# A new instruction order, and a tail with pieces of its own, in a one-core transformer layer

## The chip, the core and the metric

The kernel runs on one core of one Trainium2 chip. A core has five engines, each with an in-order queue of its own: TensorE (PE in the profile, its weight loads PEld), VectorE (DVE), ScalarE (ACT), GpSimd (POOL) and SyncE (SP), which issues the DMAs here. The metric is device time in microseconds; lower is better.

## The reference

One decoder layer on 512 tokens of width 1024, everything in float32:

```
def reference(x, ...):
    h = rms_norm(x, attn_pre_norm)
    mix = hybrid_mixer(h, ...)              # see below
    x = x + rms_norm(mix, attn_post_norm)
    h = rms_norm(x, ffn_pre_norm)
    f = (silu(h @ w_gate) * (h @ w_up)) @ w_down
    return x + rms_norm(f, ffn_post_norm)   # rms_norm: x * rsqrt(mean(x*x) + 1e-6) * gain
```

`hybrid_mixer` multiplies h by one input projection `w_in` (after which the queries and keys get rotary embedding) and feeds two groups of heads: four differential heads (the difference of two causal softmax maps of 64 dimensions, applied to 128-wide values) and eight heads of native sparse attention (NSA) in two groups, each the gated sum of a branch over 31 compressed blocks, a branch over selected blocks and a window branch. At this length every block is selected and the window covers all, so the last two are causal softmaxes over the same scores' shape with different keys. The groups are joined and go through `w_out`.

## The kernel before, in words

TensorE multiplies in a rounded 32-bit type (fp32r). So that the result keeps float32 precision, every operand is split into a high part (rounded, a ScalarE copy or POOL cast) and a low part (the rest, a VectorE or POOL subtraction), and a product is three matmuls: high by high, low by high, high by low. An operand is ready for TensorE only after the load, the high part and the low part, in that order.

There is no scheduler at run time. The program is a list of small steps, each of which appends a few instructions to the engines' queues. Two strings of names give the order of the list: `PLAN` (1384 steps) for the normalisation, input projection and attention, and `PLAN_NORM` for the output projection's norm, the feed-forward part and the end. The position of a name decides where its instructions stand in each queue, and since a queue is in order, an instruction that waits holds back all that follow it on that engine. SP's DMAs are in such a queue too.

Names in `PLAN` that matter below: `xL3`, `xH3`, `xl3` load chunk 3 of x (transposed, line L385), and make its high (L389) and low part (L393); `bL0.0` loads a block of `w_in` (L503), into a buffer that an earlier block must have left; `F m.c.k` is one product piece of the projection (L517). For the heads, D is a differential and N an NSA head: `LD` loads queries (qst, L617), `K` loads keys (`load_keys`, kst, L624), `S` are score products on TensorE (two matmuls, L867 and L868), `Q` adds the causal mask by a matmul (L873), `X` takes the row maximum (L877, VectorE), `E` the exponentials (L881, ScalarE), `R` the reciprocal of the sums and `g` the gate, `M` scales the weights by gate and reciprocal on POOL (L1050), `T` transposes them on TensorE (L898), `H` and `L` make the parts of the transposed (L908, L911), `V` are the products with the values. `SC`, `TC`, `HC` are scores (scc, L1027 with its mask at L1029), transposes (trc, L1069) and copy (pct, L1073, ScalarE) of the compressed branch. The digits behind the letters are branch or map and tile. `RB` broadcasts a row by TensorE, and `v1p2.0` is a piece of the value projection (L650). So N3S12 is a score product of NSA head 3 and D2S12 one of differential head 2; N4K0 loads the first keys of NSA head 4 over those of head 3.

In the feed-forward part gate and up projections go by a scheme with sums of operand blocks (Strassen's), so that weights are added on VectorE before the split: `load_ff.f.g` loads the gate weights of feature group f, `sum_ff.f.n` forms the sums of weights (n = 1 is L1376, e<-wraw; 2 is L1378; 3 is L1383; 4 is L1381), `high_ff`, `low_ff` split them (L1396 on ScalarE; L1404 on VectorE), `h3.s4`, `l3.s3` and the like make the high and low part of sums of activations (L1332 and L1335, in the profile "rope"), and `block.f.p` is one product of the scheme (L1419). `c0` and so on are sums of activations (L1361), `act` lines (L1438) belong to the SwiGLU of the tiles before.

In the end `down` multiplies by `w_down` (L1641), 22 feature tiles for each quarter of the output: 128 tokens (i) by 512 columns (c). The last quarter is i = 1, c = 0 (`LAST` is 1). For each i follow on the result: `last_sum` (adds the bank to the part kept so far, L1657), `last_square` (ScalarE with a running sum, L1672), `last_mean` (L1678), `last_root` (the reciprocal root of the mean square by Ln and Exp on ScalarE and a Newton step on VectorE, L299 to L308), `last_gain` (times the gain, L1687) and `last_row` (times the root, plus the residual, L1691, and the DMA to the output, L1692). The last quarter's sum and square are taken in two halves of 256 columns, out of one bank.

Of the kernel before, what the change touches and what calls it, by code (L numbers as in the profile page):

```python
# [47 lines left out]
bl1.0 F5.1.1 F4.1.1 F1.2.1 bl2.0 F0.0.1 F0.1.1 xL2 F0.2.1 xH2 F3.0.1 F5.2.1 F3.1.1 F3.2.1 F3.0.2 xl2 F2.0.2 F2.1.2  # L48
F4.0.2 bL3.0 bh3.0 F5.0.2 F0.0.2 F0.1.2 F1.0.2 F5.1.2 F0.2.2 F3.1.2 F4.2.2 xL3 xH3 F0.0.3 F5.2.2 F3.2.2 F3.0.3
F1.1.2 F1.2.2 F1.0.3 bL0.0 bh0.0 bl3.0 F3.1.3 F4.0.3 F0.1.3 xL0 xl3 xS3 F5.2.3 F5.0.3 F4.2.3 F3.2.3 F2.2.2 F2.0.3  # L50
F0.2.3 xS1 xA3 bl0.0 xH0 F0.0.0 F2.1.3 F2.2.3 xl0 F4.1.2 bL4.0 F5.2.0 bh4.0 F5.1.3 bl4.0 F1.1.3 F1.2.3 xS0 F3.0.0
F3.1.0 xL4 xH4 F4.1.3 F0.1.0 F0.2.0 F5.0.4 xl4 F2.0.0 F5.0.0 F2.1.0 F5.1.0 F5.2.4 F3.2.0 F4.0.4 F3.0.4 F3.1.4 F4.2.4
bL5.0 xL5 bh5.0 bl5.0 xH5 F4.0.5 F5.0.5 cL xl5 F2.2.0 F4.0.0 F3.2.4 xS2 F3.0.5 cc F5.1.4 xL6 xH6 xL7 F3.1.5 xl6
F4.2.0 xH7 xl7 F1.0.0 F4.1.0 KP1 F1.1.0 F1.2.0 xA2 F2.0.4 F2.1.4 F1.0.4 F0.0.4 F2.2.4 xS5 xS7 rL2 F0.1.4 F0.2.4
bL7.0 bh7.0 F4.2.7 F0.0.5 F0.1.5 F0.2.5 F1.1.4 xA5 F1.2.4 xA7 F1.0.5 F1.1.5 F1.2.5 bl7.0 F5.1.7 xS4 xA4 xS6 xA6
F5.2.5 rL0 F4.1.4 bL6.0 bh6.0 F4.2.6 rL3 xA1 rs F4.2.5 F2.0.5 KW10 bl6.0 F4.1.6 F2.1.5 F5.1.5 F2.2.5 F2.0.6 rn rb
# [25 lines left out]
N3Q02 N3X03 N2E01 W4h D1L2 D0RB N1M11 D0ML LW1 N1T02 N1H02 v1p3.0 N2R0 N2X13 N2E11 N2g0 N0O1 N0O2 N2E13 N1T01 N2CM
N2R1 N2g1 N1L02 N1H01 N1L01 N1T00 N2M00 N1H00 D1V0 D1V1 D1V2 D1O3 N1L00 N1TC N1HC N1M10 N3SC N3E03 N1T11 N2M03 pW4
D2LD0 D2S00 N3S01 N3Q01 D2Q00 N3CX N1H11 N3CA N3CE N3S1 D2X01 N3CS N2M11 N3S0 N2PH D1SQ N2M12 N4LD D2E01 W6b N2M02
D2S01 N3X02 N3E02 N1L11 N2M10 N3Q0 N3X00 N3X10 N2M01 D2X00 D2Q01 N3Q1 N3X01 N1T10 N1H10 N1L10 N2M13 N3E01 v1p3.1
D0OH N1T12 N1H12 D2S02 N3X11 N1L12 N3E00 v1a3 N3R0 D0OL D2X02 N1V00 v1d3 N1VC N3E10 N1V01 N3g0 N3CM D2E02 N1V02
N3M01 N2T00 N2H00 N2PL N3M03 N1V10 N1V11 N1V12 D2Q02 N2TC N2L00 N4SC D2LD1 D2X03 D2E00 N3PH N2T11 N4CX D2S10 N3M00
W6a N1O1 D2E03 D2S11 N2H11 D2Q10 N1O2 N2L11 D2X11 D2Q11 D2X10 N2T01 N3S11 N3E11 N3S12 W4l N3M02 N2H01 N2HC N4K0
D2S12 N2T10 D2Q12 D2E10 D2X12 N3Q12 N2L01 N3Q11 N3X12 N2T02 N3PL D2E11 D2X13 v1p2.0 W1h N2H02 N2L02 N2H10 N2L10
N2T12 N4CA D2E12 D2E13 D2R N3E12 N3X13 D2g D2MX0 D2MX3 N3E13 N3R1 N2H12 v1p2.1 N4S01 N2V00 N2V01 v1a2 D2MX2 N1OH  # L90
N4K1 N3g1 N4CE N3M13 N2VC N3M12 N2L12 N2V02 N4Q01 N3TC N3T01 N3HC N3H01 N4X02 v1d2 N4S1 D2MX1 N4S0 N3M10 N4S11 N3L01
# [162 lines left out]
def hybrid_block_kernel(  # L254
# [1400 lines left out]
    def last_sum(i, c, h=None):  # L1655
        u = piece(part[i, c], h)
        dve.tensor_tensor(u, u, piece(quarter(i, c), h), OP.add)  # L1657
# [303 lines left out]
```

## Time and profile before

| | |
|---|---|
| three runs | 627.74, 629.05, 627.74 us (median 627.74) |
| profiled execution | 628.53 us, span 626.7 us |
| TensorE | busy 614.8 us, 98% of the span |
| VectorE | 548.8 us, 88% |
| ScalarE | 374.6 us, 60% |
| POOL | 100.3 us, 16%, nearly all of it between 100 and 310 us |
| DMA | 98.41 MB, mean 157 GB/s |

The span runs from the first to the last instruction that the profiler saw; the execution's own time has some 2 us around it. The timeline gives for each instruction (or run of like ones, "x4") the start, the duration, engine, line, operation and tiles, and in brackets how long the engine had been idle before it and for what it waited. Matmuls overlap: their durations are longer than the distance of their starts, so that for TensorE the distances are read. "issue" as a reason means that nothing on another engine shows why the instruction had not begun; often it is a DMA.

### The profile page before, as it was taken

The page shows a single profiled execution, that of the slowest core. Times are in us where ns is not written, and L with a number is a line of the kernel's source. Part 1 is how long each engine was busy: PE and PEld are TensorE (multiplying, and loading weights), DVE is VectorE, ACT ScalarE, POOL GpSimd, SP SyncE. Part 2 cuts the span into 40 slices and gives each one's busy share as a digit, 9 for nine tenths or more (in the row PEclk, how much of TensorE's full clock was granted, in tenths as well). Part 3 has the DMA queues.
Part 4 walks back from the last instruction along what each step waited for, and adds up shares of the span by engine and source line. Part 5 has one row for each costly group of instructions (what it writes and reads, how often), then busy time and mean ns, then how long its engine had stood idle before and what let it go on. Part 6 is the DMA issues. An engine that isn't in the chain of part 4 may idle for free.

```text
span 626.7 us, 10975 instructions
## 1 busy us (share of the span) xinstructions
PE 614.8 (98%) x4066; PEld 558.9 (89%) x4066; DVE 548.8 (88%) x967; ACT 374.6 (60%) x783; POOL 100.3 (16%) x151
## 2 busy tenths in 40 slices
PE   9999999999999999999999999999999999999995
PEld 6888888899889989889989999999999998888884
DVE  4799798888889875999989998798999899999877
ACT  5536455558888977477574644464554656576522
POOL 0030000115878878200000000000000000000000
PEclk9999999999999999999999999999999999999998
DMA  8748887655242311545243443434442454666503
GB/s 241 247 134 287 287 283 242 224 185 169 69 153 84 135 35 35 200 169 201 65 139 101 135 136 101 135 121 150 139 136 96 132 189 147 206 220 220 172 27 134
DMA packets 38181, 98.41 MB, mean 157 GB/s; under 512 B 4208, under 2 KB 11504, under 8 KB 37232
## 3 DMA queue, kind: packets, MB, share of 16 engines
q1 hardware_dynamic: 38128, 97.72, 47.6%
q8 instruction: 32, 0.52, 0.3%
q14 instruction: 21, 0.17, 0.1%
HBM read 82.10 MB, written 15.60 MB: 156 GB/s over the span
## 4 chain that ended last, share of the span: by engine, by line
PE 85%; DVE 9%; ACT 3%; DMA 1%; issue 1%; DVEq 0%; ACTq 0%
PE yz L1419 26%; PE acc L1493 14%; PE fm L534 9%; PE fm L517 5%; PE x L1419 4%; PE v L650 4%; PE tr L898 3%; PE avn L1081 3%; PE acc L1641 3%; PE g L650 2%; PE sc L867 2%; PE sc L868 2%; PE mixp L1152 1%; DMA wraw<-in_wg 1%; PE cmp L749 1%; PE av L959 1%
## 5 line engine op out<-in xcount | busy, mean ns | idle before, releaser
L881 ACT ACTIVATE p<-sc,nm 128x384 f32<-128x384 f32 (+3 forms) x96 | 50.3, 529 | 12.8 <-DVE nm L877 11.0
L1419 PE MATMUL yz<-rope,wbh 128*128 128x256 f32 x352 | 49.2, 282 | 1.6 <-DVE rope L1335 1.6
L877 DVE TENSOR_REDUCE nm<-sc 128x1 f32<-128x384 f32 (+3 forms) x96 | 43.1, 482 | 6.5 <-PE sc L873 4.8
L1419 PEld LDWEIGHTS yz<-rope,wbh 128*128 128x128 f32 x352 | 44.9, 188 | 1.8 <-DVE rope L1335 1.8
L1050 POOL TENSOR_TENSOR p<-p,l 128x384 f32<-128x384 f32 (+3 forms) x64 | 44.8, 727 | 0.9
L911 DVE TENSOR_TENSOR ptl<-tr,pth 128x384 fp32r<-128x384 f32 (+1 forms) x60 | 34.7, 595 | 6.9 <-ACT pth L908 6.4
L908 ACT ACTIVATE pth<-tr 128x384 fp32r<-128x384 f32 (+1 forms) x60 | 30.4, 527 | 7.4 <-PE tr L898 6.7
L1404 DVE TENSOR_TENSOR wel<-e,weh 128x1024 fp32r<-128x1024 f32 x22 | 26.8, 1220 | 7.3 <-ACT weh L1396 4.2
L1396 ACT ACTIVATE weh<-e 128x1024 fp32r<-128x1024 f32 x22 | 23.3, 1057 | 14.7 <-DVE e L1378 7.7
L1396 ACT ACTIVATE wbh<-wraw 128x1024 fp32r<-128x1024 f32 x22 | 23.2, 1056 | 13.4 <-DVE wraw L1383 9.2
L898 PE MATMUL tr<-ident,p 128*128 128x128 f32 x200 | 29.8, 274 | 0.8 <-ACT pct L1073 0.5
L1396 ACT ACTIVATE whi<-wraw 128x1024 fp32r<-128x1024 f32 x22 | 23.1, 1055 | 11.4 <-DMA wraw<-in_wg 10.5
L1542 ACT ACTIVATE whi<-wraw 128x1024 fp32r<-128x1024 f32 x20 | 21.1, 1059 | 13.7 <-PE acc L1493 6.3
L1419 PE MATMUL yz<-rope,wbl 128*128 128x256 f32 x176 | 28.1, 282 | 0.0
L1404 DVE TENSOR_TENSOR wbl<-wraw,wbh 128x1024 fp32r<-128x1024 f32 x22 | 26.7, 1218 | 0.8 <-PE yz L1419 0.6
L1404 DVE TENSOR_TENSOR wlo<-wraw,whi 128x1024 fp32r<-128x1024 f32 x22 | 26.8, 1217 | 0.2 <-ACT whi L1396 0.2
L1548 DVE TENSOR_TENSOR wlo<-wraw,whi 128x1024 fp32r<-128x1024 f32 x20 | 24.1, 1219 | 1.5 <-ACT whi L1542 1.5
L1449 ACT ACTIVATE us<-yz 128x512 f32<-128x512 f32 x22 | 13.0, 593 | 19.4 <-PE yz L1419 19.3
L867 PE MATMUL sc<-kst,qst 128*128 128x512 f32 (+3 forms) x64 | 23.0, 370 | 1.3 <-issue 0.8
L898 PEld LDWEIGHTS tr<-ident,p 128*128 128x128 f32 x200 | 22.3, 141 | 1.9 <-issue 0.6
L1419 PEld LDWEIGHTS yz<-rope,wbl 128*128 128x128 f32 x176 | 23.9, 188 | 0.0
L868 PE MATMUL sc<-kst,qst 128*128 128x512 f32 (+3 forms) x64 | 21.6, 343 | 0.0
(379 smaller groups left out, 1996.2 us busy)
## 6 DMA issues: line engine op xcount, KB each, us to landing
wraw<-in_wg SPq DMA_DIRECT2D x24, 512.0 KB, 3.7
wraw<-in_wu SPq DMA_DIRECT2D x22, 512.0 KB, 3.5
wraw<-in_wd SPq DMA_DIRECT2D x22, 512.0 KB, 4.1
qk<-rope SPq DMA_DIRECT2D x7, 1024.0 KB, 5.3
kst<-qk SPq DMA_DIRECT2D x24, 256.0 KB, 4.8
wraw<-in_wf SPq DMA_DIRECT2D x10, 512.0 KB, 4.7
wraw<-in_wo SPq DMA_DIRECT2D x8, 512.0 KB, 5.1
qst<-qk SPq DMA_DIRECT2D x16, 256.0 KB, 3.6
```

The costliest lines, as they stand in the source:

```text
L534: pe.matmul(st["fm", m], fms[m][w][:, k * P:(k + 1) * P], xx[k], start=(c == 0 and k == 0), stop=(c == 2 and k == NK - 1))
L650: pe.matmul(pts[i], xx[k][:, i * P:(i + 1) * P], ws[c][wi][:, off:off + n], start=(m == 0), stop=(m == 3 * NK - 1))
L867: pe.matmul(sv[i], lhs, kk[:, 0, :w], start=(n == 0), stop=False, skip_group_check=True)
L877: dve.tensor_reduce(nm[i], sv[i], AX.X, OP.max, negate=True)
L881: act.activation(pp[i], sv[i], AF.Exp, bias=nm[i], accum_out=hs["l"][:, row, i:i + 1])
L898: pe.transpose(tr[:, n * P:(n + 1) * P], pp[i][:, j * P:(j + 1) * P], ident)
L911: dve.tensor_tensor(part(u, 1), tv[u], f32(part(u, 0)), OP.subtract)
L1050: pool.tensor_tensor(p, p, hs["l"][:, 1 + br, i:i + 1].to_broadcast(list(p.shape)), OP.mult)
L1396: act.activation(t[0], w[src], AF.Copy)
L1404: dve.tensor_tensor(t[1], W[f][PARTS[n][0]], f32(t[0]), OP.subtract)
L1419: pe.matmul(o, W[f][w][wi][:, k * P:(k + 1) * P], hop[h][hi][:, k * HS:(k + 1) * HS], start=(n < 3 and m == 0), stop=(m == 11), skip_group ...
L1493: pe.matmul(acc[t], a[x][:, t * P:(t + 1) * P], b[y], start=(first and n == 0), stop=(last and n == 2))
```

## The change

Four edits come together.

1. Steps 31 to 868 of `PLAN` are put in another order. The steps are the same. This reaches from the second chunk of x to N4K0; from `D2Q12` on the orders are equal.
2. In `PLAN_NORM` the step `l3.s3` moves ahead of `sum_ff.4.1`.
3. The last reciprocal roots: one ScalarE function `Abs_reciprocal_sqrt` in place of Ln and Exp, and the Newton step in another form, with one VectorE operation fewer and a ScalarE copy beside it. The table that is loaded for it changes.
4. The end of the last quarter. `down` for it stops at feature tile 19, and tiles 20 and 21 are multiplied in halves of 256 columns into two banks of their own (`down_piece`). The sum becomes a 512-wide addition for the first bank and a 256-wide one for each piece. `last_gain` of half 1 of `LAST` goes to POOL. The last row goes out in three pieces (512, 256 and 256 columns), the last of them by a DMA that ScalarE issues. Squares of tile 0 are written into the same scratch as those of `LAST`, and the order at the end is another.

```diff
+    def rsqrt_last(outp, ss, scale, rest):
+        v, y, t, z = (cpool.tile([P, 1], F32, tag=f"rr{j}c", name="rr", bufs=2) for j in range(4))
+        act.activation(y, ss, AF.Abs_reciprocal_sqrt, bias=rest, scale=scale)
+        dve.tensor_scalar(v, ss, scale, rest, OP.mult, OP.add)
+        dve.scalar_tensor_tensor(t, y, y, v, OP.mult, OP.mult)
+        act.activation(z, y, AF.Copy, scale=-0.5)
+        dve.scalar_tensor_tensor(outp, t, 3.0, z, OP.subtract, OP.mult)
...
-                      start=(first and n == 0), stop=(f == NF - 1 and n == 2))
+                      start=(first and n == 0), stop=(f == (NF - 3 if (i, c) == (LAST, 0) else NF - 1) and n == 2))
+
+    def down_piece(f, h):
+        o = HS + LAST % 2 * P
+        for n, (a, wi) in enumerate(((0, 0), (1, 0), (0, 1))):
+            pe.matmul(accs[7][h][:, :HS], ffx[f][a][:, o:o + P], piece(oa[f]["w"][wi][:, CS[0]], h),
+                      start=(f == NF - 2 and n == 0), stop=(f == NF - 1 and n == 2))
...
     def last_sum(i, c, h=None):
         u = piece(part[i, c], h)
-        dve.tensor_tensor(u, u, piece(quarter(i, c), h), OP.add)
+        dve.tensor_tensor(u, u, quarter(i, c) if h is None else accs[7][h][:, :HS], OP.add)
...
-        rsqrt_mean(r, wc[i][0][:, j:j + 1], 1.0 / D_MODEL, "c", wc[i][0][:, 3:4])
+        rsqrt_last(r, wc[i][0][:, j:j + 1], 1.0 / D_MODEL, wc[i][0][:, 3:4])
...
-        dve.tensor_tensor(out_tiles(i)[1 + c], part[i, c], gains[2][:, CS[c]], OP.mult)
+        u = out_tiles(i)[1 + c]
+        (nc.gpsimd if (i, c) == (LAST, 1) else dve).tensor_tensor(u, part[i, c], gains[2][:, CS[c]], OP.mult)
...
-    def last_row(i, c):
-        u = wc[i][1 + c]
-        dve.scalar_tensor_tensor(u, u, wc[i][3], x2[i][:, CS[c]], OP.mult, OP.add)
-        nc.sync.dma_start(out[i * P:(i + 1) * P, CS[c]], u)
+    def last_row(i, c, h=None):
+        u = piece(wc[i][1 + c], h)
+        dve.scalar_tensor_tensor(u, u, wc[i][3], piece(x2[i][:, CS[c]], h), OP.mult, OP.add)
+        (nc.scalar if h else nc.sync).dma_start(piece(out[i * P:(i + 1) * P, CS[c]], h), u)
...
-snap_2.3 sx.1 block.2.3 h3.s3 load_ff.4.u low_ff.3.b block.3.3 sum_x.3 load_ff.4.g high_ff.4.a sum_ff.4.1 l3.s3
+snap_2.3 sx.1 block.2.3 h3.s3 load_ff.4.u low_ff.3.b block.3.3 sum_x.3 load_ff.4.g high_ff.4.a l3.s3 sum_ff.4.1
...
-table.natural_log_exp_and_others cut_b.3.0.1 load_b.8 cut_b.4.1.0 cut_b.4.1.1 cut_b.4.2.1 load_s4.4 cut_b.8.2.0
+table.abs_reciprocal_sqrt_and_small cut_b.3.0.1 load_b.8 cut_b.4.1.0 cut_b.4.1.1 cut_b.4.2.1 load_s4.4 cut_b.8.2.0
```

Behind the first functions all line numbers of the new kernel are larger, by 8 in the middle and by up to 15 at the end.

TensorE at the end of the reordered stretch, before: the scores of NSA head 3 (kst_1117), those of differential head 2 (kst_2083), then transposes.

```order
L867 MATMUL sc_2293<-kst_1117,qst_1878 128x384
L868 MATMUL sc_2293<-kst_1117,qst_1878 128x384
L867 MATMUL sc_2298<-kst_1117,qst_1878 128x512
L868 MATMUL sc_2298<-kst_1117,qst_1878 128x512
L867 MATMUL sc_2308<-kst_2083,qst_2245 128x512
L868 MATMUL sc_2308<-kst_2083,qst_2245 128x512
L898 MATMUL tr_2311<-ident_83,p_1960 128x128
```

The same place in the new order (head 3's keys are kst_1056, those of differential head 2 kst_1745):

```order
L875 MATMUL sc_2280<-kst_1056,qst_1908 128x384
L876 MATMUL sc_2280<-kst_1056,qst_1908 128x384
L875 MATMUL sc_2283<-kst_1745,qst_2148 128x512
L876 MATMUL sc_2283<-kst_1745,qst_2148 128x512
L875 MATMUL sc_2287<-kst_1056,qst_1908 128x512
L876 MATMUL sc_2287<-kst_1056,qst_1908 128x512
L906 MATMUL tr_2298<-ident_83,p_1972 128x128
```

The pair D2S12 has gone from behind to ahead of N3S12, which is the last to read head 3's keys.

VectorE in the feed-forward part, before: around the sums of the weights of group 4 (e<-wraw waits for their load) and the low part that `l3.s3` makes (rope<-s_4132).

```order
L1335 TENSOR_TENSOR rope<-s_4075,rope 128x4x128
L1438 TENSOR_TENSOR act_4166<-x_3894,snap 128x256
L1404 TENSOR_TENSOR wbl<-wraw,wbh 128x1024
L1438 TENSOR_TENSOR act_4196<-x_3970,snap 128x256
L1376 TENSOR_TENSOR e<-wraw 128x512
L1335 TENSOR_TENSOR rope<-s_4132,rope 128x4x128
L1378 TENSOR_TENSOR e<-wraw,e 128x512
L1404 TENSOR_TENSOR wlo<-wraw,whi 128x1024
```

The same place in the new order:

```order
L1343 TENSOR_TENSOR rope<-s_4075,rope 128x4x128
L1446 TENSOR_TENSOR act_4166<-x_3894,snap 128x256
L1412 TENSOR_TENSOR wbl<-wraw,wbh 128x1024
L1446 TENSOR_TENSOR act_4196<-x_3970,snap 128x256
L1343 TENSOR_TENSOR rope<-s_4132,rope 128x4x128
L1384 TENSOR_TENSOR e<-wraw 128x512
L1386 TENSOR_TENSOR e<-wraw,e 128x512
L1412 TENSOR_TENSOR wlo<-wraw,whi 128x1024
```

The two neighbours rope<-s_4132 and e<-wraw have changed places.

VectorE's last instructions before, from the row of half 0 of tile 0 on (c_7131 is half 1 of the last tile, c_7172 half 0):

```order
L1657 TENSOR_TENSOR c_7131<-c_7131,acc_6630 128x512
L1691 SCALAR_TENSOR_TENSOR uf<-uf,rs,x2b_7094 128x512
L1687 TENSOR_TENSOR uf<-c_7131,gain 128x512
L1691 SCALAR_TENSOR_TENSOR uf<-uf,rs,x2b_7094 128x512
L1657 TENSOR_TENSOR c_7172<-c_7172,acc_6698 128x256 x2
L1678 TENSOR_SCALAR ss<-ss 128x1 x2
L1687 TENSOR_TENSOR uf<-c_7172,gain 128x512
L300 TENSOR_SCALAR rr<-ss 128x1
L303 SCALAR_TENSOR_TENSOR rr<-rr 128x1
L307 TENSOR_SCALAR rr<-rr 128x1
L308 TENSOR_TENSOR rs<-rr 128x1
L1691 SCALAR_TENSOR_TENSOR uf<-uf,rs,x2b_7335 128x512 x2
```

And in the new order:

```order
L1671 TENSOR_TENSOR c_7131<-c_7131,acc_6630 128x512
L1671 TENSOR_TENSOR c_7172<-c_7172,acc_6698 128x512
L1671 TENSOR_TENSOR c_7172<-c_7172,acc_6679 128x256
L1692 TENSOR_SCALAR ss<-ss 128x1
L1671 TENSOR_TENSOR c_7172<-c_7172,acc_6680 128x256
L1702 TENSOR_TENSOR uf<-c_7172,gain 128x512
L1692 TENSOR_SCALAR ss<-ss 128x1
L299 TENSOR_SCALAR rr<-ss 128x1
L300 SCALAR_TENSOR_TENSOR rr<-rr 128x1
L302 SCALAR_TENSOR_TENSOR rs<-rr 128x1
L1706 SCALAR_TENSOR_TENSOR uf<-uf,rs,x2b_7335 128x512
L1706 SCALAR_TENSOR_TENSOR uf<-uf,rs,x2b_7335 128x256 x2
```

The gain of half 1 has left the queue (it is POOL's), the sum of half 0 is three operations, the gain of half 0 stands ahead of the second mean, and the rows of the tile before stand ahead of these.

More of the change, by code (lines that the diff above doesn't have):

```diff
@@ L47 @@
 wu xL1 gc xH1 xl1 bL1.1 bh1.1 F2.0.1 F4.2.1 F1.0.1 F4.0.1 bl1.1 bL1.0 bh1.0 F5.0.1 F1.1.1 F2.1.1 F2.2.1 bL2.0 bh2.0
[L48 to L56, printed above, removed]
@@ L82 @@
[L82 to L91, printed above, removed]
@@ new lines @@
+N2S12 N0VC N0V10 N3S0 D1H2 N0V11 N1M11 N0L12 N0V12 N2X11 N2Q12 N2X10 N2E10 D1T1 N2S11 D1L0 D1V0 D1L2 N0O1 N1M10 D1H1
+N1M03 N0O2 D1L1 N2E11 N3SC N3Q0 N2CS N2E01 N2X13 N2E13 N3CX D1V1 D1V2 D1O3 N2Q11 N1TC N1HC N3X10 N2R0 N2X12 N2g0
+N2M03 N3X00 D0RB D0ML N1T00 N2CM N2E12 N2R1 N2g1 N1T10 N1H10 N1T01 v1p3.0 N1H01 N3E10 N1L01 D2S01 N1T02 D2Q01 N3CA
+D0OH N1T12 N1L10 N2M02 v1p3.1 N2M11 D1SQ N3CE N3CS D2S00 N3E00 N3S01 N3S1 N1H02 N1L02 N1H12 N1L12 N2M00 N2PH N2PL
+v1a3 D2LD1 D2X02 N1H00 N1L00 v1d3 D2E02 N3S02 N1T11 N1H11 N3Q01 N3X02 N3E02 N3Q02 N3Q1 N3X01 N3E01 D2Q00 N1V00 N1VC
@@ new lines @@
+N1V01 D2S02 N3X03 N3E03 N1L11 N1V02 N2M13 N2M12 D2X01 D2Q02 D2X03 N2T11 D2X00 N2H11 D0OL D2E03 N1V10 N1V11 N1V12
+N1O1 N2M01 N2M10 N2L11 N2T00 N2H00 N3R0 N3X11 N3E11 N3g0 N2T01 N2H01 N3CM N1O2 N2L00 D2S10 D2S11 N4LD N4SC N4CX N2TC
+D2Q11 D2Q10 N3S11 D2S12 N3M01 N3S12 D2X11 D2E01 N2HC D2X10 N2T10 N3M03 W6b W6a N3PH N3M00 D2E00 N4K0 N3M02 D2Q12
+D2E10 D2X12 N3Q12 N2L01 N3Q11 N3X12 N2T02 N3PL D2E11 D2X13 v1p2.0 W1h N2H02 N2L02 N2H10 N2L10 N2T12 N4CA D2E12 D2E13
+D2R N3E12 N3X13 D2g D2MX0 D2MX3 N3E13 N3R1 N2H12 v1p2.1 N4S01 N2V00 N2V01 v1a2 D2MX2 N1OH N4K1 N3g1 N4CE N3M13 N2VC
@@ L1663, in out_tiles @@
             wc[i] = [cpool.tile([P, 4], F32, tag="ssc", name="ss", bufs=NT), sslot("uf", F32), sslot("uf", F32)]
-            if i == LAST:
+            if not junk and i in (0, LAST):
                 junk.extend(sslot("uj", BF16) for _ in range(2))
@@ L1670, in last_square @@
         j = (1 - c) + (h or 0)
-        sq = junk[c] if i == LAST else wc[i][1 + c].bitcast(BF16)
+        sq = junk[c] if i in (0, LAST) else wc[i][1 + c].bitcast(BF16)
         act.activation(piece(sq[:, :SEQ], h), piece(part[i, c], h), AF.Square,
@@ L1794, in hybrid_block_kernel @@
     at(-1.0, table, "silu_and_others")
-    at(te + 6.0, table, "natural_log_exp_and_others")
+    at(te + 6.0, table, "abs_reciprocal_sqrt_and_small")
     D = 3 * 2 * 0.228
```

125 lines of the change are left out of this document (70 added, 55 removed).

## The prediction

> **What bounds the kernel now.** I read the page first (shares, chain, costliest groups), then the busy time by stretches, then the timeline of TensorE wherever a stretch showed idle time, and the engines that it waits for there. The page and the stretches:
>
> ```profile
> PE 614.8 (98%) x4066; PEld 558.9 (89%) x4066; DVE 548.8 (88%) x967; ACT 374.6 (60%) x783; POOL 100.3 (16%) x151
> PE 85%; DVE 9%; ACT 3%; DMA 1%; issue 1%; DVEq 0%; ACTq 0%
> ```
>
> ```profile
> 0.00:160.00 160.00, 158.78 (x924) 137.76 (x925) 133.00 (x257) 91.11 (x201) 22.18 (x38) 1.00 0.70 229
> 160.00:190.00 30.00, 28.20 (x213) 25.69 (x212) 25.62 (x60) 25.64 (x74) 24.50 (x37) 1.00 0.33 109
> ```
>
> TensorE is the bound: 98% busy, 85% of the chain. So an edit can pay in two ways only: it closes a hole in TensorE's row, or it shortens the 7 us after its last matmul. The first 160 us have 1.22 us of idle (mostly the start, ahead of the first product), and the next 30 us have 1.80; the new order of the attention part covers these 190 us. That already bounds the gain of the large edit: some 2 us, not 20. Its harm has no such bound.
>
> **The new order of the attention part.** Holes are read from start to start, since a matmul's end is modelled. Three are inside the stretch that is reordered or just behind it:
>
> ```profile
> 167.05 0.23 PE L1029 MATMUL scc<-cmask_b,ident_b 128*128 128x128 bf16 x1
> 167.79 0.52 PE L898 MATMUL tr<-ident,p 128*128 128x128 f32 x3 [0.51 <-ACT pct L1073]
> ...
> 177.44 0.23 PE L1029 MATMUL scc<-cmask_b,ident_b 128*128 128x128 bf16 x1
> 177.51 0.50 PE L898 MATMUL tr<-ident,p 128*128 128x128 f32 x3
> 178.44 0.30 PE L867 MATMUL sc<-kst,qst 128*128 128x128 f32 x1 [0.43 <-ACT p L881]
> ```
>
> ```profile
> 180.19 0.40 PE L867 MATMUL sc<-kst,qst 128*128 128x512 f32 x1
> 180.66 0.39 PE L867 MATMUL sc<-kst,qst 128*128 128x512 f32 x1
> ...
> 181.13 0.60 PE L898 MATMUL tr<-ident,p 128*128 128x128 f32 x4
> ...
> 183.50 0.49 PE L898 MATMUL tr<-ident,p 128*128 128x128 f32 x3
> 183.75 0.72 PE L650 MATMUL v<-whi,xh 128*128 128x256 f32 x4
> 184.30 0.64 PE L650 MATMUL v<-whi,xl 128*128 128x256 f32 x4
> 184.78 0.64 PE L650 MATMUL v<-wlo,xh 128*128 128x256 f32 x4
> 186.21 0.41 PE L867 MATMUL sc<-kst,qst 128*128 128x384 f32 x1 [0.79 <-issue]
> ```
>
> ```profile
> 180.85 2.37 SPq L624 DMA_DIRECT2D kst<-qk  x4
> ```
>
> A (167 us): from the mask product to the transposes 0.74, against 0.07 for the same pair at 177.44: 0.67 lost to ScalarE's copy of the transposed compressed weights (L1073), with only the scc group between. In the new order N1TC is followed by D0RB and by N1T00, N1T10 and N1T01, and the scc group N3SC has gone ahead of it. I take this hole as closed, -0.67 (0 if ScalarE is as late for the next transposes).
> B (178 us): 177.51 to 178.44 is 0.93, where three transposes take 0.25 (183.50 to 183.75): 0.68 lost to an exponential that still holds a bank. Its neighbours change places; I count half, -0.34 (0 to -0.68).
> C (186 us): the keys of NSA head 4 (N4K0, four DMAs on SP) can only go when N3S12, the pair of 180.19, has read the old ones: SP issues at 180.85, and TensorE stands at 186.21, 1.43 after 184.78 where such a group takes 0.48 (184.30 to 184.78): 0.95 lost. "issue" hides a DMA here. Now the diff shows that D2S12, the pair of 180.66 to 181.13, stands ahead of N3S12 instead of behind it. All else between N3S12 and N4S01 is the same work, so 0.47 us of cover leaves this gap and the hole should grow from 0.95 to 1.42: +0.47, on the path. Only a faster load would undo it.
> Elsewhere the old order has next to no holes in 160 us, so the new one can only make some. What was moved furthest upstream is the load of x's chunk 3, behind block bL0, which waits for a buffer. It goes out where chunk 0 did:
>
> ```profile
> 6.71 0.58 PE L517 MATMUL fm<-xh,whi 128*128 128x512 f32 x1
> ```
>
> ```profile
> 8.60 0.72 ACT L389 ACTIVATE xh<-xraw,gc 128x512 fp32r<-128x512 f32 x1
> ```
>
> ```profile
> L385 SPq DMA_DIRECT2D xraw<-in_xT x1: 542/542/542, 8.1 to 8.1; - x1
> DMA to landing us min/median/max: 4.1/4.1/4.1
> ...
> xraw<-in_xT SPq DMA_DIRECT2D x8, 256.0 KB, 5.4
> ```
>
> The rows: TensorE's first product, the rounding of a chunk, the load of chunk 0, and the median of all eight. Issued at 8.1 and landed at 12.2, rounded by ScalarE in 0.72 until 12.95; the first product with it is the 30th after the start at 6.71, which at 0.23 a product falls at about 13.4. So it just fits, and with the median landing of 5.4 TensorE would wait 0.8. For all such new waits I take +0.3, with bounds 0 and +2.0 (a handful of holes of the size of A to C).
>
> **The swap of l3.s3 and sum_ff.4.1.** VectorE, ScalarE and SP around 318 us, and TensorE there:
>
> ```profile
> 318.09 0.69 DVE L1376 TENSOR_TENSOR e<-wraw 128x512 f32<-128x512 f32 x1 [1.87 <-DMA wraw<-in_wg]
> 318.70 0.68 DVE L1335 TENSOR_TENSOR rope<-s,rope 128x512 fp32r<-128x512 f32 x1
> 319.90 1.22 DVE L1404 TENSOR_TENSOR wlo<-wraw,whi 128x1024 fp32r<-128x1024 f32 x1
> ```
>
> ```profile
> 317.25 0.63 PE L1419 MATMUL yz<-rope,wbh 128*128 128x256 f32 x4
> 319.44 0.74 PE L1419 MATMUL yz<-rope,wbh 128*128 128x256 f32 x4 [1.56 <-DVE rope L1335]
> 321.44 0.64 PE L1419 MATMUL yz<-x11h,wlo 128*128 128x256 f32 x4
> 321.93 0.75 PE L1419 MATMUL yz<-rope,wbh 128*128 128x256 f32 x5
> ```
>
> ```profile
> 317.99 1.06 ACT L1396 ACTIVATE whi<-wraw 128x1024 fp32r<-128x1024 f32 x1 [2.28 <-DMA wraw<-in_wg]
> ```
>
> VectorE stands 1.87 us before L1376 for a weight load, with the rope operand that TensorE needs behind it in the queue. Moved ahead it runs at 316.2 to 316.9, while VectorE idles anyway, and TensorE goes on at 317.72. But of the hole of 1.72 (317.25 to 319.44 less 0.47) only a part is won, because the block's second half needs the same load. TensorE would finish its two rope groups at 318.7 and wait until 319.1 for whi, which ScalarE can't start before the landing; then x11h and x11l on whi until 320.0, and wlo, on VectorE now at 319.3 (one operation of 0.60 less ahead of it) to 320.5, costs another 0.5. The group after it starts at 321.0 instead of 321.93: -0.9 (bounds -0.3, if a later load holds the next block up, and -1.7).
>
> **The tail.** Last matmul at 619.25, then VectorE and ScalarE alone:
>
> ```profile
> 615.62 0.15 DVE L1678 TENSOR_SCALAR ss<-ss 128x1 f32<-128x1 f32 x1 [0.19 <-ACT uf L1672]
> 615.70 0.68 DVE L1687 TENSOR_TENSOR uf<-c,gain 128x512 f32<-128x512 f32 x1
> ...
> 619.68 0.75 DVE L1657 TENSOR_TENSOR c<-c,acc 128x256 f32<-128x256 f32 x2
> 620.81 0.68 DVE L1687 TENSOR_TENSOR uf<-c,gain 128x512 f32<-128x512 f32 x1
> 621.08 0.30 ACT L299 ACTIVATE rr<-ss 128x1 f32<-128x1 f32 x1
> ...
> 622.36 1.41 DVE L1691 SCALAR_TENSOR_TENSOR uf<-uf,rs,x2b 128x512 f32<-128x512 f32 x2
> ```
>
> ```profile
> L1050 POOL TENSOR_TENSOR p<-p,l 128x384 f32<-128x384 f32 (+3 forms) x64 | 44.8, 727 | 0.9
> ```
>
> ```profile
> L1140 POOL TENSOR_TENSOR wl<-wraw,wh 128x512 fp32r<-128x512 f32 x10 | 12.7, 1286 | 0.2
> ...
> out<-uf SPq DMA_DIRECT2D x4, 256.0 KB, 2.0
> ```
>
> VectorE has no gap from 614 on, so what counts is its queue. The gain of half 1 goes to POOL (-0.60, as a 512-wide operation takes from start to start, 318.09 to 318.70); the sum over tiles 18 and 19 is a new 512-wide addition (+0.60): nil together. The first root now follows both gains without the 0.19 of idle, so VectorE comes to it at 616.1 instead of 616.3, and it is a little shorter: the rows behind it start about 0.24 earlier. The halves of the last sum no longer wait for each other's matmuls but still for VectorE: I get the last 256-wide sum done at 620.3, gain until 620.9, mean until 621.2, the root function 621.5 (0.30, as Ln's), then two VectorE steps of a quarter us, with the Copy beside the first, where the stretch between 621.38 and 622.36 held Exp and three steps: rows from 622.0 instead of 622.36, three pieces in the same 1.4. Gain 0.3. The last store is issued by ScalarE; it and two queues are not in the trace: bounds -0.6 and +0.5, I take -0.3. The new bank of pieces costs twelve 256-wide products at 0.12 for six at 0.23, nil. The table load stays one of three.
> Weighed against this: the Trainium skill ("DMA: Bandwidth & Descriptors", Anatomy of one DMA) gives a transfer's time as 2.0 us and bytes over 436e9. By that, an estimate from its figures, a last piece of 128 KB instead of 256 KB saves another 0.3 us and the whole would be 626.0. The trace's 2.0 us for 256 KB doesn't bear the sum out (2.6 by the rule), so I don't count it.
>
> **The sum.** -0.67 - 0.34 + 0.47 + 0.3 - 0.9 - 0.3 = -1.4 us. The profiled execution took 628.53 us with a span of 626.7, 0.8 above the median of the runs shown (627.74, up to 629.05), so I set the change against the median: 626.3 us.
>
> **Rivals.**
> No measurable change (627.2, between 626.5 and 629.0): the swap gives 0.3 to 0.6 since the wait for its load turns up at the next block, A only moves, C grows. For it: TensorE catches up with the same load twice within 3 us. Against: nothing after 320 us shows a hole of that size. Chance 0.36. A measurement of this kernel can tell about 0.2%, 1.26 us, from no change, so my forecast lies just past that edge.
> The tail's POOL gain. POOL would start it when the sum of half 1 ends, about 618.9, and by 1.29 (L1140) end at 620.2, 0.1 us before VectorE's last gain. If the two exclude each other, each 0.1 us that POOL is later is lost once, at most 1.29: by 0.3 the tail's gain is gone and the time is 626.6. The Trainium skill ("SBUF — State Buffer", Who interferes with whom) states such a lock: a VectorE operation with both inputs in SBUF and a GpSimd operation that reads SBUF block each other for a whole instruction. No row of the tail can show it, since POOL does nothing there now. Chance that it costs over 0.3: 0.1, counted within the other cases.
> Slower (629.5): POOL's scaling of the NSA weights. It is busy 24.50 of 30 us in 160 to 190. N2T11 now comes 9.6 us of TensorE work behind N2's last exponential, with six scalings between (at 0.73 from L1050, 4.4 us) and the reciprocal and gate, which I put at 1: some 4.2 us to spare. If POOL is further behind than that, TensorE waits for the rest, one for one; the sign turns when the backlog passes 4.2 + 1.4, and at 7.4 it is 1.8 slower. For it: POOL has only 5.5 idle us here. Against: most scalings were emitted well ahead. Chance 0.12.
> The change doesn't do what it says in the tail, where VectorE stays the chain and the new addition eats what POOL takes over; that is in the sum already. All holes closed with no new one would give -0.67 - 0.68 - 0.9 - 0.6, and +0.47: 625.4; chance 0.14, within faster.
>
> **Chances and range.** Forecast and its better case 0.52 together, no change 0.36, slower 0.12. The range goes from 624.6, the better case with the whole hole of 1.7 at 318 us, to 628.6, where the new waits reach 2.0 and the swap gives 0.3.
>
> **What would show it.** The swap: L1335's second rope operation near 316.2, and TensorE with two short waits, for whi and wlo, instead of 1.56. C: the wait for kst about 0.5 longer. A: no wait for pct near 167. The start: no wait for x's chunk 3 near 13.4. Tail: rows from 1.0 us after the last mean, no wait for POOL. I am wrong if TensorE shows new waits of more than 1 us before 190 us, or if the gain at 318 us is gone by 330.

## The result, and the profile after

The changed kernel takes 624.32 us in the median of six runs (622.59 to 625.94) against 628.51 us for the kernel before (six runs, 627.74 to 629.05): a ratio of 0.9933, 95% interval 0.9918 to 0.9948, so 4.2 us faster (3.3 to 5.2). The profiled execution is the fastest of the six, 622.59 us with a span of 620.5; against the trace of before (628.53, span 626.7) it shows 6.2 us, more than the medians do. Every ratio below is to the kernel before, run beside the kernel in question on the same chip. Two of the executions below were disturbed (669.9 us with the new order alone, and 1228.5 us, the profiled one, in the kernel with distances by phase); the times given leave them out, and that profile is not read.

The page's busy times and then the busy time by stretches after the change (the first stretch from 20 us on), to be laid beside those of before:

```profile
PE 610.4 (98%) x4072; PEld 555.3 (89%) x4072; DVE 548.8 (88%) x964; ACT 374.1 (60%) x783; POOL 101.6 (16%) x152
```

```profile
20.00:160.00 140.00, 139.56 (x844) 124.19 (x843) 122.52 (x234) 78.85 (x183) 25.63 (x37) 1.00 0.66 225
160.00:190.00 30.00, 29.93 (x234) 28.18 (x233) 27.29 (x65) 26.51 (x79) 22.15 (x35) 1.00 0.34 107
```

The 1.80 us of idle in 160 to 190 us have become 0.07. But TensorE's *busy* time has fallen by 4.4 us as well, with the same work (six 512-wide products have become twelve 256-wide ones, hence 4072 for 4066). No edit of the four takes a product away; this is what the prediction had no term for. Where it went is seen when the trace is cut at four instructions of TensorE: the first product of the projection, the first and the last Strassen product (L1419, 1848 of them), and the last matmul.

| us | first product at | to first Strassen product | Strassen products | to last matmul | to the end |
|---|---|---|---|---|---|
| before | 6.71 | 280.01 | 224.84 | 107.69 | 7.45 |
| after | 6.25 | 278.32 | 220.52 | 108.03 | 7.38 |
| difference | -0.46 | -1.69 | -4.32 | +0.34 | -0.07 |

The first column went from 5.9 to 7.4 us over the traces below whatever the kernel. The third is the surprise. Its Strassen products, before (start, duration; four matmuls in a row):

```profile
363.30 0.64 PE L1419 MATMUL yz<-x22h,dh 128*128 128x256 f32 x4
363.77 0.63 PE L1419 MATMUL yz<-x22l,dh 128*128 128x256 f32 x4
364.24 0.64 PE L1419 MATMUL yz<-x22h,dl 128*128 128x256 f32 x4
364.72 0.64 PE L1419 MATMUL yz<-xs1h,weh 128*128 128x256 f32 x4
365.19 0.64 PE L1419 MATMUL yz<-xs1l,weh 128*128 128x256 f32 x4
```

And the same products after:

```profile
359.88 0.62 PE L1427 MATMUL yz<-x22h,dh 128*128 128x256 f32 x4
360.33 0.62 PE L1427 MATMUL yz<-x22l,dh 128*128 128x256 f32 x4
360.78 0.62 PE L1427 MATMUL yz<-x22h,dl 128*128 128x256 f32 x4
361.24 0.64 PE L1427 MATMUL yz<-xs1h,weh 128*128 128x256 f32 x4
361.71 0.64 PE L1427 MATMUL yz<-xs1l,weh 128*128 128x256 f32 x4
```

Four x22 products took 0.47 us from start to start and now take 0.45 (113 ns each instead of 118); four xs1 products take 0.47 to 0.48 in both. Nothing waits. What tells the two kinds apart is where their operands lie: the root function has four columns instead of three, each in two slots of 32 bytes, so the pool of constants grew by 64 bytes per partition and all pools behind it (weights, s, r) lie 64 bytes further on; pools a and b, laid out from the other end, do not move. The distance of the stationary operand's start from the moving operand's, modulo 256 bytes (from the addresses in the two programs), and the mean time from start to start:

| moving, stationary (pools) | products | before: distance, ns | after: distance, ns |
|---|---|---|---|
| xs1, xs2 with weh, wel (a, a) | 528 | 0, 119.6 | 0, 119.7 |
| x22 with dh, dl (a, s) | 264 | 128, 118.8 | 192, 115.0 |
| x11, x12 with whi, wlo (b, weights) | 528 | 128, 118.8 | 192, 115.4 |
| rope with wbh, wbl (r, a) | 528 | 128, 118.7 | 64, 116.0 |

Only the pairs whose distance changed got faster. The granted TensorE clock doesn't tell the two traces apart: its mean is 0.997 of full speed before and 0.996 after. Theory P: the distance of the two operands sets the pace, and the gain is mostly this. Theory L: the pace is set by how a block of products happens to begin, and the order or chance changed that.

### The profile page after: what moved, and what is told of

The parts are those of the page before. It is cut to its first block, busy times and chain, and to the rows that moved or that the text cites. A ratio compares the mean times of both kernels' runs of the same rounds, so it can differ in the third digit from the quotient of the medians.

```text
span 620.5 us, 10979 instructions
## 1 busy us (share of the span) xinstructions
PE 610.4 (98%) x4072; PEld 555.3 (89%) x4072; DVE 548.8 (88%) x964; ACT 374.1 (60%) x783; POOL 101.6 (16%) x152
## 4 chain that ended last, share of the span: by engine, by line
PE 94%; DVE 2%; DMA 1%; ACT 1%; POOL 1%; issue 0%; DVEq 0%; ACTq 0%
PE yz L1427 30%; PE acc L1501 14%; PE fm L542 9%; PE mix L1174 5%; PE x L1427 5%; PE fm L525 4%; PE tr L906 4%; PE acc L1649 3%; PE avn L1089 3%; PE g L658 2%; PE v L658 2%; PE sc L875 2%; PE sc L876 2%; PE mixp L1160 1%; PE cmp L757 1%; PE av L967 1%
## 5 line engine op out<-in xcount | busy, mean ns | idle before, releaser
L889 ACT ACTIVATE p<-sc,nm 128x512 f32<-128x512 f32 (+3 forms) x96 | 50.4, 530 | 16.2 <-DVE nm L885 15.7
L1702 POOL TENSOR_TENSOR uf<-c,gain 128x512 f32<-128x512 f32 x1 | 1.3, 1282 | 359.2 <-DVE c L1671 359.2
L1058 POOL TENSOR_TENSOR p<-p,l 128x256 f32<-128x256 f32 (+3 forms) x64 | 45.2, 732 | 1.0
L875 PE MATMUL sc<-kst,qst 128*128 128x512 f32 (+3 forms) x64 | 22.7, 365 | 0.0
```

The costliest lines, as they stand in the source:

```text
L875: pe.matmul(sv[i], lhs, kk[:, 0, :w], start=(n == 0), stop=False, skip_group_check=True)
L889: act.activation(pp[i], sv[i], AF.Exp, bias=nm[i], accum_out=hs["l"][:, row, i:i + 1])
L1058: pool.tensor_tensor(p, p, hs["l"][:, 1 + br, i:i + 1].to_broadcast(list(p.shape)), OP.mult)
```

## The experiments

**64 bytes alone, and everything but the 64 bytes.**

```diff
     eps = cpool.tile([P, 1], F32, name="eps")
+    shift = cpool.tile([P, 16], F32, name="shift")
+    dve.memset(shift[:, :1], 0.0)
```

> The kernel before with one unused tile of 64 bytes per partition among the constants and nothing else; every tile of the left-hand pools (weights, s, r) lies 64 bytes further on, as in the changed kernel. Theory P (placement): the 256-wide products whose moving and stationary operands lie in pools of different sides go from 118.8 to about 115.5 ns start to start, so 2 to 4 us faster than before, with the holes near 167, 178, 186 and 318 us as they were. Theory L (the pace is set by how each block of products happens to begin, or by the order): within 0.5 us of before and a pace of 118.8 to 119.6 ns for all pairs of pools.

Measured: 625.37 us against 628.15, ratio 0.9961 (0.9944 to 0.9978): 2.5 us faster (1.4 to 3.5) by an unused tile. The pairs' paces are 119.7, 114.9, 115.3 and 116.2 ns, in the order of the table, and the x22 products run as in the changed kernel:

```profile
365.24 0.62 PE L1421 MATMUL yz<-x22h,dh 128*128 128x256 f32 x4
365.69 0.62 PE L1421 MATMUL yz<-x22l,dh 128*128 128x256 f32 x4
366.14 0.62 PE L1421 MATMUL yz<-x22h,dl 128*128 128x256 f32 x4
```

The Strassen products take 220.69 us, 4.15 less than in the trace of before; the other stretches of this trace are longer by 0.86 in sum. The holes of the old order are still there (waits of 0.5, 0.45 and 1.2 us at 168, 179 and 187 us).

The other way round, on the changed kernel:

```diff
-        v, y, t, z = (cpool.tile([P, 1], F32, tag=f"rr{j}c", name="rr", bufs=2) for j in range(4))
+        v, y, t, z = (cpool.tile([P, 1], F32, tag=f"rr{j}c", name="rr", bufs=2 if j < 2 else 1) for j in range(4))
```

> The changed kernel with its four small root columns in six slots instead of eight, so that all other tiles lie where they lay in the kernel before. Theory P: the pace is back at 118.8 ns and above, and 2 to 2.5 us of the gain are left (order 1.7, swap 0.6, tail 0 to 0.3), so 2 to 4 us slower than the changed kernel. Theory L: as the changed kernel, 4 us faster than before.

Measured: 627.01 us, ratio to before 0.9987 (0.9974 to 1.0001), paces 118.6 to 119.6 ns, and four x22 products take 0.47 to 0.48 us again:

```profile
362.95 0.63 PE L1427 MATMUL yz<-x22h,dh 128*128 128x256 f32 x4
363.42 0.64 PE L1427 MATMUL yz<-x22l,dh 128*128 128x256 f32 x4
363.90 0.64 PE L1427 MATMUL yz<-x22h,dl 128*128 128x256 f32 x4
```

So order, swap and tail together are worth 0.8 us (0 to 1.6), less than the 2 to 2.5 that I still expected of them, and the place of the tiles the rest of the 4.2, some 3.4, beside the 2.5 (1.4 to 3.5) that it gave alone. The order as a cause falls, and chance with it: same order, same tail, other distances, other pace. What is left of theory L is taken up below.

**All distances in one kernel, and distance 0.** Pool a's slots 4128 instead of 4096 bytes apart:

```diff
-        return A.tile([P, D_MODEL], dt, tag="f", name=name, bufs=NF4)
+        return A.tile([P, D_MODEL + 8], dt, tag="f", name=name, bufs=NF4)[:, :D_MODEL]
```

> The changed kernel with the sixteen feed-forward tiles of pool a laid out 4128 bytes apart instead of 4096, so that their start takes all eight multiples of 32 bytes modulo 256, and each pair of stationary and moving operand has one of eight distances. Theory P (the distance of the two operands' starts modulo some power of two sets the pace): a table of pace by distance, about 119.6 ns at 0, 118.8 at 128, 115 to 116 at 64 and 192, whatever the pools. Theory Q (it is the pools or the time that matter, not the distance): one pace for each pair of pools at all distances.

Measured: 625.10 us in a single execution, and by distance 118.6 ns at 0, 118.5 at 32, 116.7 at 64, 118.2 at 96, 118.2 at 128, 118.3 at 160, 117.1 at 192, 117.7 at 224. Pairs inside pool a reach 117.2 at 64 and 192 as the pairs across pools do: it is the distance, not the pool. Nor is it where one operand lies by itself: distance 64 gave 116.5, 117.1 and 117.3 ns with the moving operand's start at 64, 32 and 96 bytes modulo 128, while distance 0 with both at 64 gave 118.6. The spread is smaller than between whole layouts; why is not shown.

Another 64 bytes of constants on the changed kernel (the unused tile of the first experiment, with `eps`), which makes every Strassen distance 0:

> The changed kernel with another unused tile of 64 bytes among the constants, so that the left-hand pools lie 128 bytes further than in the kernel before and most pairs start at distance 0 modulo 256. Theory P: the pace of all pairs is 118.5 to 120 ns as at distance 0 in pool a, and the gain of placement is gone: 0 to 1 us faster than before. Rival: any move away from the old place helps, as fast as the changed kernel.

Measured: 627.78 us, ratio 0.9985 (0.9972 to 0.9999). All 1848 run at 120.0 ns in the mean, to be read off the rows:

```profile
360.41 0.64 PE L1429 MATMUL yz<-x22h,dh 128*128 128x256 f32 x4
360.89 0.64 PE L1429 MATMUL yz<-x22l,dh 128*128 128x256 f32 x4
361.37 0.64 PE L1429 MATMUL yz<-x22h,dl 128*128 128x256 f32 x4
361.85 0.64 PE L1429 MATMUL yz<-xs1h,weh 128*128 128x256 f32 x4
```

The forecast holds for the pace and missed one thing: the stretch from the last Strassen product to the last matmul took 106.21 us instead of 108.03. The 512-wide products of that stretch are fastest in this layout. Before, and in this kernel:

```profile
564.16 0.40 PE L1493 MATMUL acc<-whi,tbh 128*128 128x512 f32 x1
564.40 0.40 PE L1493 MATMUL acc<-whi,tbl 128*128 128x512 f32 x1
564.63 0.39 PE L1493 MATMUL acc<-wlo,tbh 128*128 128x512 f32 x1
564.86 0.39 PE L1493 MATMUL acc<-whi,tbh 128*128 128x512 f32 x1
```

```profile
556.40 0.39 PE L1503 MATMUL acc<-th,sh 128*128 128x512 f32 x1
556.63 0.39 PE L1503 MATMUL acc<-th,sl 128*128 128x512 f32 x1
556.86 0.39 PE L1503 MATMUL acc<-tl,sh 128*128 128x512 f32 x1
557.08 0.39 PE L1503 MATMUL acc<-th,sh 128*128 128x512 f32 x1
```

Three steps of the first take 0.70 us, three of the second 0.68; by pairs of pools the mean is 228 to 232 ns before, where the distances are mixed (228 to 229 for the pairs at distance 0, 232 for those at 128), and 226.7 at distance 0 throughout (227.7 for one pair of pools).

**The new order alone, twice, and the changed kernel without it.** `PLAN` of the changed kernel in the kernel before:

> The kernel before with the new order of the attention part alone (tiles where they were). If the two traces split rightly, 1.3 to 2.2 us faster than before: the holes at 167, 178 and 186 us gone, the one at 318 us as before, the pace of the 256-wide products as before. If order and pace hang together (theory L): 3 to 5 us faster.

Measured: 628.30 us, ratio 1.0001 (0.9986 to 1.0017), twelve runs from 625.91 to 630.40. The holes at 167, 178 and 186 us are gone (29.68 us of 30 busy in 160 to 190) and two others have come; for the larger one, TensorE's row and ScalarE's name the cause:

```profile
73.30 2.12 PE L534 MATMUL fm<-xh,whi 128*128 128x512 f32 x8 [1.09 <-ACT whi L521]
```

```profile
70.95 1.06 ACT L737 ACTIVATE whi<-wraw 128x1024 fp32r<-128x1024 f32 x1 [3.11 <-DMA wraw<-in_vw]
72.19 1.06 ACT L521 ACTIVATE whi<-wraw 128x1024 fp32r<-128x1024 f32 x1 [0.18 <-DMA wraw<-in_wf]
```

ScalarE stands 3.11 us before the split of the value compression's weights, and the split that the projection needs is queued behind. In the changed kernel's trace, in the same order, that load lands in time:

```profile
68.65 1.06 ACT L745 ACTIVATE whi<-wraw 128x1024 fp32r<-128x1024 f32 x1 [0.23 <-DMA wraw<-in_vw]
70.36 1.06 ACT L529 ACTIVATE whi<-wraw 128x1024 fp32r<-128x1024 f32 x1 [0.65 <-DMA wraw<-in_wf]
```

The load went out at 63.3 and 63.5 us in the two, among nine DMAs within 6 us, and the two loads of its kind took 8.1 and 6.3 us in the median to land. So the order alone was run again:

> The new order alone at the old places, once more, since its first trace showed two weight loads landing late (1.26 us at 71.8 us, 0.74 at 89.9) that the same order does not show in the changed kernel. If that was chance: 1.5 us less between the first product and the first Strassen product, and a median 0.5 to 1.5 us below before. If it belongs to the order: the same holes at the same places, and no gain.

Measured: 627.14 us, ratio 0.9972 (0.9955 to 0.9989); the hole at 72 us is 0.66 this time, and another at 139 us is 0.73. And the changed kernel with the old order:

> The changed kernel with the attention part's old order. If the order is worth what the profile of the changed kernel shows (the holes at 167, 178, 186 us closed), 1.5 to 2 us slower than the changed kernel, 0.4% faster than before. If the new order's own late loads eat that on average, as its run alone suggests, the same as the changed kernel, 0.6 to 0.7% faster than before.

Measured: 624.87 us, ratio to before 0.9946 (0.9925 to 0.9967), beside 0.9933 with the new order. From the first product to the first Strassen product, eight traces with the old order took 279.3 to 280.4 us (mean 279.8), seven with the new one 277.9 to 280.8 (mean 279.1). The new order is some 1.6 us better in the four traces in which its loads land in time (277.9 to 278.6) and no better or worse in the three in which they don't (279.6 to 280.8), 0.8 us on average of these traces. The pairs of medians (0.55 here, 0.53 and 0.82 below, -0.15 and 1.29 alone) lie within their noise but for the last, whose interval is clear of no change.

**The swap alone, twice.**

```diff
-snap_2.3 sx.1 block.2.3 h3.s3 load_ff.4.u low_ff.3.b block.3.3 sum_x.3 load_ff.4.g high_ff.4.a sum_ff.4.1 l3.s3
+snap_2.3 sx.1 block.2.3 h3.s3 load_ff.4.u low_ff.3.b block.3.3 sum_x.3 load_ff.4.g high_ff.4.a l3.s3 sum_ff.4.1
```

> The kernel before with l3.s3 ahead of sum_ff.4.1 and nothing else. TensorE's wait of 1.56 us gives place to two of 0.6 and 0.4: 0.6 to 0.9 us faster. Rival: the next load takes it back by 330 us, 0 to 0.3 us.

> The swap alone once more, since in its first trace TensorE waited 0.9 + 0.4 us for the high and low parts of the same weight load, against 0.4 in all with the changed kernel's other parts. If the landing of that load varies by chance: a wait between 0.4 and 1.3 us and a gain between 0.2 and 1.2 us. If it is fixed by the code around: again 1.3 us and a gain of 0 to 0.3 us.

Measured: 627.72 us, ratio 0.9998 (0.9988 to 1.0008), then 627.40, 0.9986 (0.9974 to 0.9998). TensorE's wait of 1.56 for rope is gone in both; it waits 0.9 and 0.4 us for whi and wlo in the first, 0.4 and 0.4 in the second. The wait that takes its place is for the same load, whose landing varies. So does the wait that the swap removes: in the five readable traces without the swap it is 0.7 to 1.6 us (1.3 on average), and in the ten with it the two waits sum to 0.2 to 1.3 (0.8 on average). The 1.56 of the trace before lies near the upper end.

**The tail alone.** The old order, the old places, the swap undone in the changed kernel:

> The changed kernel with the old order of the attention part, with l3.s3 back behind sum_ff.4.1, and with the root columns in six slots: the new tail alone at the old places. By the profiles, from the last matmul to the end 7.4 us against 7.45 before: 0 to 0.3 us faster. Rival: the tail holds what the order and the swap did not give, 0.6 to 1 us faster.

Measured: 628.63 us, ratio 1.0013 (0.9996 to 1.0030); from the last matmul to the end 7.40 us against 7.45. The tail gives nothing that can be measured here.

**All Strassen products at 64 or 192, with both orders.** Each slot of pool a 128 bytes longer, weh and wel 64 bytes into theirs:

```diff
-    def f4(name, dt=F32):
-        return A.tile([P, D_MODEL], dt, tag="f", name=name, bufs=NF4)
+    def f4(name, dt=F32, off=0):
+        return A.tile([P, D_MODEL + 32], dt, tag="f", name=name, bufs=NF4)[:, off:off + D_MODEL]
...
-            t = pair_of("w" + n)
+            t = tuple(f4(f"w{n}{h}", F32R, 16 if n == "e" else 0) for h in "hl")
```

> The changed kernel with pool a's tiles 4224 bytes apart and the sums of gate and up weights (weh, wel) starting 64 bytes into theirs, so that all 1848 Strassen products have their two operands 64 or 192 bytes apart modulo 256. Theory P (distance sets the pace): the 528 products that stayed at 119.7 ns go to 115 to 116 ns and the others gain by the even pace, 2 to 4 us faster than the changed kernel (1.0% to 1.3% faster than before); the down products, whose distances get more mixed, lose at most 0.5 us. Rival: only the pairs across pools follow the distance, and no more is to be had.

> The kernel just named with the attention part's old order. If the new order is worth its 1.5 us between the first product and the first Strassen product, 1.5 us slower than that; if late loads take it back in half of the executions, 0.5 to 0.8 us.

Measured: 622.97 us, ratio 0.9921 (0.9895 to 0.9947) with the new order and 623.50, 0.9920 (0.9905 to 0.9936) with the old. The xs products went from 119.7 to 116.4 ns, about as forecast (115.8 at 64, 116.8 at 192), but x22's rose from 115.0 to 117.5 and the mean only fell from 116.8 to 116.2. The x11 and x12 products kept their distance of 192 and went from 115.4 to 116.6, so a product's own distance is not all.

The means hide two paces. In the changed kernel's trace, the groups of four products at distance 64 or 192 run either at 113 to 114 ns each (167 of 320 groups) or at 116 to 119 (153), and none between. Two groups at distance 192, in this trace:

```profile
384.09 0.63 PE L1427 MATMUL x<-x12l,whi 128*128 128x256 f32 x4
384.56 0.63 PE L1427 MATMUL x<-x12h,wlo 128*128 128x256 f32 x4
...
387.90 0.62 PE L1427 MATMUL yz<-x11h,whi 128*128 128x256 f32 x4
388.36 0.62 PE L1427 MATMUL yz<-x11l,whi 128*128 128x256 f32 x4
388.81 0.62 PE L1427 MATMUL yz<-x11h,wlo 128*128 128x256 f32 x4
```

Four products take 0.47 us in the first and 0.45 to 0.46 in the second. It is not chance: 313 of 318 groups run at the same pace in the trace with the attention part's old order. In the layout of this experiment, with every product at 64 or 192, only 157 of 447 groups are at the fast pace; before, at distance 0 or 128, no group is under 116. So the distance decides whether the fast pace occurs, and which of the two a stretch runs at is settled by something that stays the same from run to run, as theory L had it in part; what it is, is not shown.

The two kernels of this experiment have the fastest medians of the study, 0.8 to 1.4 us under the changed kernel's; the intervals overlap with its 0.9933, so that they beat it is likely and not shown.

**Each phase with its own distances.** The kernel of distance 0 with pool r and the four tiles of pool b moved:

```diff
+    rpad = R.tile([P, 16], F32, name="rpad", bufs=1)
+    dve.memset(rpad[:, :1], 0.0)
...
-... else B.tile([P, D_MODEL], dt, tag=n, name=n, bufs=1) for n in (name + "h", name + "l"))
+... else B.tile([P, D_MODEL + 64], dt, tag=n, name=n, bufs=1)[:, 16:16 + D_MODEL] for n in (name + "h", name + "l"))
```

> The kernel shifted by 128 with pool r and the four tiles of pool b moved 64 bytes, so that 1056 of the Strassen products have distance 192 (64 the other way round) and the other 792 and all down products distance 0. Theory P, each phase by its own distances: Strassen products of about 116 ns in the 1056 and 119.5 ns in the 792, 221 to 222 us for that phase against 225.5 at distance 0, and the down products at 226.7 ns as there, 106.2 us for what follows against 108.0 of the changed kernel: 1.0 to 1.2% faster than before. Rival: the pace of the down products hangs on something else that the even layout had, and comes back to 229 ns with pool b moved: 0.7% faster.

> The kernel just named with the attention part's old order, the third pair that differs in the order alone. From the pairs so far (0.55, 0.53 us for the new order, and 0.15 against and 1.3 for it when it stood alone): 0.5 us slower than the kernel just named, with less spread from run to run.

Measured: 624.99 us, ratio 0.9948 (0.9930 to 0.9966) with the new order, 625.81, 0.9959 (0.9941 to 0.9977) with the old. The trace with the old order shows 117.9 ns in the 1056 moved products, 120.0 in the 792 others, and 226.7 to 228.1 ns in the 512-wide ones, 106.27 us for their stretch. So each phase follows its own distances. The 256-wide gain was half of what I expected: all 257 groups of four at distance 192 run at the slower of the two paces, 117 to 119 ns, and none at 113. Why is not shown.

## Why the prediction was wrong

It forecast 626.3 us, 1.4 less than before, and 624.6 at the lowest. Measured was 624.32, which is 4.2 less than the kernel before that ran beside it (628.51, where I set out from 627.74). The sign was right; the size was not, since the largest term was missing.

The step that failed is the one that says that an edit can pay in two ways only, by closing a hole in TensorE's row or by shortening the 7 us after its last matmul. It read "98% busy" as a floor and put a change of TensorE's busy time at nothing, without a reason. That time fell from 614.8 to 610.4 us. The same step shows in the part on the tail, where the root's new form was counted as instructions only: its fourth column also costs 64 bytes of the constants, which move three pools, and this is worth 2.5 us alone and 3.4 as the difference between the changed kernel and the same with six slots. The starts of before could have raised the question: nearly all lie between 113 and 122 ns apart for one shape.

Without the 64 bytes the changed kernel takes 627.01 us, 0.9987 of before (0.9974 to 1.0001), which can't be told from the rival "no measurable change". So the right sign is in the main luck: it was won by a term that the prediction didn't have.

The terms that I did have, order, swap and tail, sum to -1.4 in the text; the kernel with exactly these three took 0.8 us less than before (0 to 1.6). One by one:

- A and B, -0.67 and -0.34: closed in all seven readable traces of the new order, the changed kernel's among them. A stands at 0.5 us of wait in all eight traces of the old order, as told. B comes and goes there, being absent in three of the eight.
- C, +0.47: wrong in sign. I took the load of head 4's keys to go over head 3's, and so to be released by N3S12. That holds before; the program has two slots for keys, and in the new order this load takes the one of differential head 2, which D2S12 releases, the pair that had moved ahead. Again the load goes out behind the first of the two pairs, 4.4 us of TensorE's work ahead of its use, so the cover is what it was. And the hole has closed:

```profile
178.83 0.40 PE L875 MATMUL sc<-kst,qst 128*128 128x512 f32 x1
...
183.40 0.64 PE L658 MATMUL v<-wlo,xh 128*128 128x256 f32 x4
183.88 0.34 PE L875 MATMUL sc<-kst,qst 128*128 128x384 f32 x1
```

```profile
179.49 2.37 SPq L632 DMA_DIRECT2D kst<-qk  x4
```

  In the old order TensorE goes on 0.09 us after the second of the four DMAs has landed, in all eight traces. From issue to landing, that DMA before and after:

```profile
L624 SPq DMA_DIRECT2D kst<-qk x1: 599/599/599, 181.3 to 181.3; - x1
DMA to landing us min/median/max: 4.8/4.8/4.8
...
L632 SPq DMA_DIRECT2D kst<-qk x1: 591/591/591, 180.0 to 180.0; - x1
DMA to landing us min/median/max: 3.1/3.1/3.1
```

  It takes 4.4 to 5.1 us in the eight traces of the old order and 3.1 in six of the seven of the new one (4.1 in the other), and none of these seven waits here. The prediction said that only a faster load would undo the hole, and that is what came; why the load is faster there is not shown.

- New waits, +0.3 with bounds 0 and +2.0: the right kind at other places. Not the load of x's chunk 3 but the weights at 68 to 75 us: 0 in the changed kernel's trace beyond 0.4, 2.0 in the first trace of the order alone.
- The swap, -0.9: the mechanism is as told, down to the two waits. TensorE in the changed kernel:

```profile
315.73 0.62 PE L1427 MATMUL yz<-rope,wbl 128*128 128x256 f32 x4
316.95 0.74 PE L1427 MATMUL yz<-x11h,whi 128*128 128x256 f32 x4 [0.60 <-ACT whi L1404]
...
318.54 0.74 PE L1427 MATMUL yz<-x11h,wlo 128*128 128x256 f32 x4 [0.38 <-DVE wlo L1412]
```

  The forecast was 0.4 and 0.5. Alone the swap measured 0.1 and 0.9 us by the ratios, the first of them below my lower bound of 0.3: its size hangs on the load's landing, and the hole of 1.56 that I set out from was one draw of it.
- The tail, -0.3: nothing. VectorE and ScalarE after the change:

```profile
612.83 1.28 POOL L1702 TENSOR_TENSOR uf<-c,gain 128x512 f32<-128x512 f32 x1 [359.21 <-DVE c L1671]
...
614.25 0.69 DVE L1702 TENSOR_TENSOR uf<-c,gain 128x512 f32<-128x512 f32 x1
...
615.16 0.29 ACT L298 ACTIVATE rr<-ss 128x1 f32<-128x1 f32 x1 [0.39 <-DVE ss L1692]
...
616.07 1.54 DVE L1706 SCALAR_TENSOR_TENSOR uf<-uf,rs,x2b 128x512 f32<-128x512 f32 x3
```

  From the last matmul (613.12) to the rows 2.95 us against 3.11, and the rows 1.54 instead of 1.41 since they are three. Gain and cost cancel. POOL's gain ended at 614.11, 0.14 us before VectorE's began, so the rival on it was not put to the test. The figures of the Trainium skill that the prediction weighs for the last store (2.0 us, and bytes over 436e9) stand in a section on the DMAs that GpSimd issues; these stores are SP's and ScalarE's, and nothing in the sum hangs on them.
- Of the rivals, "all holes closed with no new one" (625.4) comes nearest, by its time and not by its reason. In the changed kernel's trace no wait of TensorE is for POOL.

## What to carry to other kernels

Where an engine is 98% busy, look at the pace of its instructions and not only at its holes: tabulate start to start by operands, before and after, and look at the spread as well as at the mean. A new small tile moves every tile behind it, so an edit should be timed with the places held fixed, and a few pads of 32 to 128 bytes tried by themselves. An order that closes holes by putting loads closer together is worth what their landing allows, and only several traces tell that.

## What the runs showed of the hardware

In these kernels, the pace of a product whose weights are loaded for it alone hung on where its two operands start. The 256-wide ones took 120.0 ns in the mean with every pair at the same address modulo 256 bytes, and 118.7 at 128 apart. At 64 or 192 apart they took mostly either 113 to 114 or 116 to 119 ns, which makes means of 115 to 118 by layout. The 512-wide ones took 226.7 ns at distance 0 throughout and 228 to 233 in mixed layouts.

The Trainium skill ("TensorE: Matmul & The Clock Gate", Back-to-back issue gap) gives the isolated distance of two warm matmuls as N/2.4 + 2.5 ns, 109 and 216 ns by an estimate from it; the traces lie 4 to 11 and 11 to 17 ns above, by amounts that differ with the addresses. The 131 ns that the same section of the Trainium skill gives for a 512-wide product in a sustained stream of weight loads and matmuls isn't met here: 226.7 to 233.

Why the distance matters was not tried and stays open. Nor was it tried whether the period is 256 bytes or more.
